# Gate and up of feed-forward block 0 by Strassen's seven block products, inner tiles taken 4, 6, 6, 6 at a time

## The chip, the cores and the metric

One core of one Trainium2 chip runs the whole program. The metric is the device time in microseconds, the median of several runs. TensorE (PE) multiplies and accumulates into PSUM, in eight banks of 128 x 512 fp32; VectorE (DVE), ScalarE (ACT) and GpSimd (POOL) work element by element; SyncE (SP) issues most DMAs. Each engine takes its instructions in the order in which they were queued and waits on semaphores of the others.

## The reference

Two transformer layers run over 256 context and 256 latent tokens (512 columns here), model width 1024, hidden width 2816 (22 tiles of 128). Layer 0 mixes by retention and a state-space scan, layer 1 by latent attention. Each layer ends in a gated feed-forward block; the change is in that of layer 0:

```
h = h + m[2] * mixer(modulate(rms_norm(h), m[0], m[1]))
h = h + m[5] * swiglu(modulate(rms_norm(h), m[3], m[4]), w_gate, w_up, w_down)
def swiglu(h, w_gate, w_up, w_down):
    return (jax.nn.silu(h @ w_gate) * (h @ w_up)) @ w_down
```

The m are conditioning vectors, separate for context and latent tokens, made from a condition by another matrix. All of it is fp32.

## The kernel before, in words

Activations lie with model channels on partitions and the 512 tokens along the row: `x[k]`, k = 0 to 7. To keep fp32 accuracy, each operand is cut into a high part (`wh`, `xh`, cast by ScalarE) and a low rest (`wl`, `xl`, subtracted by VectorE, for a few units by GpSimd), and each product is three matmuls: wh·xh, wh·xl, wl·xh (`mm3`, L231 to L234).

The `Feed` object brings all weights in a fixed order: SP loads a `raw` tile of up to 1 MB (a pool of four buffers), and each unit of 512 columns is then split into `wh` (L153) and `wl` (L154). `get(la)` hands out the next unit and has the splits queued `la` units ahead. Every other tile of 512 columns comes from one pool, `heap`, of 76 buffers.

Feed-forward block 0 (`ffn`) takes the 22 inner tiles in two halves of 11. For one inner tile, two products of eight contraction steps give gate and up (2 x 8 x 3 = 48 matmuls of 512 columns; the first two tiles together, while `x` is still being made); ScalarE takes silu of the gate (`sg`, L1290), VectorE multiplies by up (L1291), and the product is cut into `hdh` and `hdl` (L227, L228). After 11 tiles, the down projection runs over the eight output tiles: 33 matmuls each, and two residual additions to `h` on VectorE (L1195, one input in PSUM). The last output tile of the block is done in two halves of the tokens by `bridge`, which also makes the next layer's norm (`ms`, L337) and its first input.

A second stream on VectorE, `vec_all`, makes the conditioning vectors of layer 1: 96 steps that multiply a row of weights by the condition and add it up (`vo`, L503). Its generator is advanced NVS = 5 steps after each inner tile; its weights come as 1 MB loads into `raw`.

The order of the instructions on each engine is set by a list scheduler from the order of the program and its own costs; only `bridge` and the start of the norm are held in program order on TensorE.

## Time and profile before

| | |
|---|---|
| median of 3 runs | 1129.97 us (1129.36 to 1131.19) |
| profiled execution | 1133.19 us |
| its span, first to last instruction | 1131.4 us |
| mean granted TensorE clock | 0.976 |
| busy: TensorE, VectorE, ScalarE, GpSimd | 1081.2 (96%), 727.7 (64%), 493.2 (44%), 203.4 (18%) us |
| block 0's gate, up and down, about | 390 to 732 us of the span |

In a row of the windows view stand the stretch, its length, the busy time of PE, weight loads, DVE, ACT and POOL with their instruction counts, the granted clock, the DMA share and GB/s. A timeline row has start, duration, engine, line, operation, output<-inputs, form and count, and in brackets how long its engine sat idle before it and what released it. Matmul durations overlap, so the price of one is the step from start to start.

### The profile page before, as it was taken

How to read it: one execution, taken by the hardware profiler on the slowest of the kernel's cores; microseconds unless marked ns; L12 is line 12 of the kernel's file. 1: busy time of each engine (PE TensorE's matmuls, PEld its weight loads, DVE VectorE, ACT ScalarE, POOL GpSimd, SP SyncE). 2: the span in 40 equal slices, each digit the busy share in tenths (PEclk: the TensorE clock that was granted, in tenths of full speed). 3: DMA queues.
4: the chain of work that ended last, by engine and by line, in shares of the span. 5: the costliest groups of instructions: out<-in, count | busy, mean ns of one | idle time of the engine just before them, and what ended most of it. 6: DMA issues, size and time to landing. Idle time of an engine off the chain costs nothing.

```text
span 1131.4 us, 17225 instructions
## 1 busy us (share of the span) xinstructions
PE 1081.2 (96%) x6537; PEld 894.4 (79%) x6537; DVE 727.7 (64%) x1547; ACT 493.2 (44%) x991; POOL 203.4 (18%) x201
## 2 busy tenths in 40 slices
PE   8899999797998899999999999989999999999997
PEld 7687666565787688888888888858988779999996
DVE  4479499756646776663275753475888767574565
ACT  4372465745333533232132322344766645453442
POOL 2123154642022300000000000342232241000001
PEclk8999999898999899999999999999999989999998
DMA  9642797012362334354135546322343563473441
GB/s 348 227 150 88 241 324 243 38 38 75 112 223 76 112 123 175 125 190 150 38 114 222 203 174 227 123 75 80 90 126 105 194 224 122 145 288 135 163 154 38
DMA packets 42962, 172.43 MB, mean 152 GB/s; under 512 B 5472, under 2 KB 7152, under 8 KB 30720
## 3 DMA queue, kind: packets, MB, share of 16 engines
q1 hardware_dynamic: 42448, 170.69, 42.8%
q8 instruction: 51, 0.84, 0.3%
q10 hardware_dynamic: 432, 0.66, 0.2%
q14 instruction: 31, 0.25, 0.1%
HBM read 167.08 MB, written 1.10 MB: 149 GB/s over the span
## 4 chain that ended last, share of the span: by engine, by line
PE 59%; DVE 6%; ACT 2%; issue 1%; DMA 1%; DVEq 0%; SPq 0%; ACTq 0%
PE g L232 18%; PE g L234 17%; PE g L233 17%; PE ya L1521 1%; DVE wl L154 1%; PE ad L427 1%; DVE xl L543 1%; ACT wh L153 1%; DVE na L542 1%; PE tp L1512 1%; ACT xh L541 1%; PE st L334 1%; DVE mx L1500 1%; PE rb L321 0%; ACT P L1503 0%
## 5 line engine op out<-in xcount | busy, mean ns | idle before, releaser
L233 PE MATMUL g<-xl,wh 128*128 128x512 f32 (+1 forms) x968 | 337.1, 349 | 10.4 <-DVE xl L543 6.8
L232 PE MATMUL g<-xh,wh 128*128 128x512 f32 (+1 forms) x968 | 336.9, 351 | 2.4 <-ACT xh L541 2.4
L234 PE MATMUL g<-xh,wl 128*128 128x512 f32 (+1 forms) x968 | 334.7, 346 | 0.0
L154 DVE TENSOR_TENSOR wl<-raw,wh 128x512 fp32r<-128x512 f32 (+2 forms) x371 | 247.9, 711 | 59.5 <-ACT wh L153 57.2
L153 ACT CAST wh<-raw 128x512 fp32r<-128x512 f32 (+3 forms) x412 | 223.7, 597 | 54.1 <-PE g L233 30.5
L233 PEld LDWEIGHTS g<-xl,wh 128*128 128x128 f32 x968 | 183.7, 190 | 37.1 <-DVE xl L543 9.5
L232 PEld LDWEIGHTS g<-xh,wh 128*128 128x128 f32 x968 | 182.7, 190 | 37.3 <-issue 10.1
L234 PEld LDWEIGHTS g<-xh,wl 128*128 128x128 f32 x968 | 183.7, 190 | 24.3 <-issue 0.8
L365 POOL TENSOR_TENSOR sq<-sq 128x256 f32<-128x256 f32 (+1 forms) x30 | 31.0, 1032 | 616.7 <-ACT sq L361 614.8
L232 PE MATMUL g<-hdh,wh 128*128 128x256 f32 (+1 forms) x363 | 120.7, 333 | 0.0
L234 PE MATMUL g<-hdh,wl 128*128 128x256 f32 (+1 forms) x363 | 120.5, 332 | 0.0
L233 PE MATMUL g<-hdl,wh 128*128 128x256 f32 (+1 forms) x363 | 120.5, 332 | 0.0
L227 ACT CAST hdh<-sg 128x512 fp32r<-128x512 f32 (+1 forms) x44 | 22.6, 513 | 174.6 <-DVE sg L1291 174.6
L1291 DVE TENSOR_TENSOR sg<-sg,g 128x512 f32<-128x512 f32 (+1 forms) x44 | 24.4, 554 | 112.1 <-PE g L234 111.5
L233 PEld LDWEIGHTS g<-hdl,wh 128*128 128x128 f32 x363 | 68.3, 188 | 7.3
L234 PEld LDWEIGHTS g<-hdh,wl 128*128 128x128 f32 x363 | 68.3, 188 | 7.3
L232 PEld LDWEIGHTS g<-hdh,wh 128*128 128x128 f32 x363 | 68.3, 188 | 7.3
L1195 DVE SCALAR_TENSOR_TENSOR h<-g,mod,h 128x256 f32<-128x256 f32 x72 | 32.3, 479 | 60.0 <-PE g L234 59.8
L154 POOL TENSOR_TENSOR wl<-raw,wh 128x512 fp32r<-128x512 f32 (+1 forms) x41 | 56.6, 1385 | 51.5 <-ACT wh L153 43.1
L1290 ACT ACTIVATE sg<-g 128x512 f32<-128x512 f32 (+1 forms) x44 | 21.5, 488 | 72.3 <-PE g L234 72.2
L361 ACT ACTIVATE sq<-h 128x256 f32<-128x256 f32 (+1 forms) x30 | 15.5, 518 | 82.0 <-DVE h L1195 69.0
L228 DVE TENSOR_TENSOR hdl<-sg,hdh 128x512 fp32r<-128x512 f32 (+1 forms) x44 | 24.6, 559 | 25.4 <-ACT hdh L227 24.9
(307 smaller groups left out, 1706.6 us busy)
## 6 DMA issues: line engine op xcount, KB each, us to landing
raw<-in_wgu_dram SPq DMA_DIRECT2D x44, 1024.0 KB, 4.8
raw<-in_wdn_dram SPq DMA_DIRECT2D x32, 704.0 KB, 4.4
vr<-in_wav_dram SPq DMA_DIRECT2D x16, 1024.0 KB, 4.9
ar<-in_wad_dram SPq DMA_DIRECT2D x12, 1024.0 KB, 6.1
ar<-in_wad_dram SPq DMA_DIRECT2D x48, 256.0 KB, 6.4
raw<-in_win_dram SPq DMA_DIRECT2D x9, 1024.0 KB, 5.1
pc<-in_wad_dram SPq DMA_DIRECT2D x32, 256.0 KB, 6.6
raw<-in_wo_dram SPq DMA_DIRECT2D x8, 1024.0 KB, 4.8
```

The costliest lines, as they stand in the source:

```text
L153: self.nc.scalar.copy(hi[:, 0:n], src)
L154: (eng or (self.nc.gpsimd if self.ns in self.pool else self.nc.vector)).tensor_tensor(lo[:, 0:n], src, hi[:, 0:n].bitcast(F32), op=ALU.sub ...
L227: ACT.copy(hi[:, c0:c1], x[:, c0:c1])
L228: DVE.tensor_tensor(lo[:, c0:c1], x[:, c0:c1], hi[:, c0:c1].bitcast(F32), op=ALU.subtract)
L232: PE.matmul(ps, wh, xh, start=first, stop=False)
L233: PE.matmul(ps, wh, xl, start=False, stop=False)
L234: PE.matmul(ps, wl, xh, start=False, stop=last)
L361: ACT.activation(q[:, c0:c1], x[:, c0:c1], AF.Square)
L365: POOL.tensor_tensor(self.acc[0][:, c0:c1], self.acc[0][:, c0:c1], q[:, c0:c1], op=ALU.add)
L1195: DVE.scalar_tensor_tensor(out=h[k][:, a:b], in0=ps[:, a:b], scalar=mod[l][:, gate * 8 + k, r:r + 1], in1=h[k][:, a:b], op0=ALU.mult, op1= ...
L1290: ACT.activation(sg[:, c0:c1], pg[:, c0:c1], AF.Silu)
L1291: DVE.tensor_tensor(sg[:, c0:c1], sg[:, c0:c1], pu[:, c0:c1], op=ALU.mult)
```

## The change

The inputs of block 0's gate and up are taken as 2 x 2 blocks: weights [gate; up] by halves of the contraction (four blocks of 512 in each `raw` tile: gate k 0 to 3 at column 0, up k 0 to 3 at 512, gate k 4 to 7 at 1024, up k 4 to 7 at 1536), activations by halves of the contraction and by alternate 128-token pieces of each stream. Inner tiles 0 and 1 are computed as before. From tile 2 on, `seven` makes seven products of 4 contraction steps and 256 columns (7 x 4 x 3 = 84 matmuls) in three PSUM banks R, X and Y: t2 into X, b11 into R, t1 onto X, t3 into Y, b21 onto R, b22 onto X, t4 onto Y. Between them ScalarE copies X (`p6`) and R (`p1`), GpSimd adds these two (`u2`), VectorE makes `u4`, both halves of `nu` (up, from Y) and `c12` (the second half of the gate, from X), and ScalarE takes silu of R and of `c12`.

Four of the seven weight blocks are sums: GpSimd makes s1 to s4 from the `raw` tile, s2 from s1 and s4 from s2. The activations' sums are made once by `combine`, on VectorE and GpSimd, and one `raw` buffer holds their high parts to the end of the block. The down projection now follows groups of 4, 6, 6 and 6 inner tiles, so that it adds to `h` four times. The conditioning stream takes three steps after each down tile in place of five after each inner tile, and loads 64 pieces of 256 KB into `heap` tiles, two ahead.

```diff
+NVS = 3
+LV = 2
+PH0 = (4, 6, 6, 6)
+LW = 4
+WSUM = ("s2", 0, "s1", "s3", 512, "s4", 1536)
...
+    def sums(self, li, key):
+        if (li, key) not in self.sum:
+            add = lambda o, a, b: self.nc.gpsimd.tensor_tensor(o[:, 0:512], a, b, op=ALU.add)
+            r = self.raw[li]
+            t = self.sum[li, key] = self.tile(key, F32)
+            if key == "s1":
+                add(t, r[:, 1024:1536], r[:, 1536:2048])
+            elif key == "s2":
+                add(t, self.sums(li, "s1"), r[:, 0:512])
+            elif key == "s3":
+                add(t, r[:, 0:512], r[:, 1024:1536])
+            else:
+                add(t, self.sums(li, "s2"), r[:, 512:1024])
+        return self.sum[li, key][:, 0:512]
...
+    def combine(x, whole):
+        keep = rawp.tile([128, 2112], F32R, tag="raw", name="tk")
...
+        for j in range(4):
+            (b11, b12), (b21, b22) = halves(whole[j]), halves(whole[j + 4])
+            ta, tb = T("ta"), T("tb")
+            DVE.tensor_tensor(pair(ta[:, 0:256]), b11, b12, op=ALU.subtract)
+            DVE.scalar_tensor_tensor(out=pair(ta[:, 256:512]), in0=b22, scalar=-1.0, in1=pair(ta[:, 0:256]), op0=ALU.mult, op1=ALU.subtract)
+            POOL.tensor_tensor(pair(tb[:, 0:256]), b22, b12, op=ALU.subtract)
+            DVE.scalar_tensor_tensor(out=pair(tb[:, 256:512]), in0=pair(ta[:, 256:512]), scalar=-1.0, in1=b21, op0=ALU.mult, op1=ALU.subtract)
+            for n, t in (("t1", ta), ("t3", tb)):
+                hi, lo = keep[:, 512 * j:512 * j + 512] if n == "t1" else T("th", F32R), T("tl", F32R)
+                ACT.copy(hi, t)
+                DVE.tensor_tensor(lo, t, hi.bitcast(F32), op=ALU.subtract)
...
+    def seven(f):
+        R, X, Y = B("wr")[:, 0:256], B("wx")[:, 0:256], B("wy")[:, 0:256]
+        def prod(ps, n, first, last=False):
+            wh, wl = feed.get(LW)
+            for k in range(4):
+                xh, xl = f[n][k]
+                w = slice(k * 128, k * 128 + 128)
+                mm3(pair(ps), wh[:, w], wl[:, w], xh, xl, first and k == 0, last and k == 3, True)
+        p, u, sg, nu = T("p"), T("u"), T("sg"), T("nu")
+        p6, p1, u2, u4 = p[:, 0:256], p[:, 256:512], u[:, 0:256], u[:, 256:512]
+        prod(X, "t2", True)
+        ACT.copy(p6, X)
+        prod(R, "b11", True)
+        ACT.copy(p1, R)
+        POOL.tensor_tensor(u2, p1, p6, op=ALU.add)
+        prod(X, "t1", False)
+        DVE.tensor_tensor(u4, X, p1, op=ALU.add)
+        prod(Y, "t3", True)
+        DVE.tensor_tensor(halves(nu)[1], pair(Y), pair(u4), op=ALU.add)
+        prod(R, "b21", False, True)
+        ACT.activation(halves(sg)[0], pair(R), AF.Silu)
+        prod(X, "b22", False, True)
+        c12 = T("c12")[:, 0:256]
+        DVE.tensor_tensor(c12, X, p1, op=ALU.add)
+        ACT.activation(halves(sg)[1], pair(c12), AF.Silu)
+        prod(Y, "t4", False, True)
+        DVE.tensor_tensor(halves(nu)[0], pair(Y), pair(u2), op=ALU.add)
+        return sg, nu
...
+        for i, n in enumerate(PH0):
+            hid = []
+            for _ in range(n):
...
+                    sg, nu = seven(f)
+                    DVE.tensor_tensor(sg, sg, nu, op=ALU.mult)
+                hid.append(split(sg, "hd"))
...
+            for k in range(8):
+                if m == 22 and k == 7:
+                    return last(hid, n, 0, 5, so)
+                residual(k, gemm(hid, n), 0, 5, BOTH)
...
+                vec_step(NVS)
```

How the order on the engines moves is seen at three places. In the rows the numbers behind `s_` tell the sums apart; lines are those of each kernel's own file.

Place 1, VectorE in the middle of a group, around one inner tile. Before:

```order
L503 ISA va 128x1
L154 TENSOR_TENSOR wl<-raw,wh 128x512 x4
L1291 TENSOR_TENSOR sg<-sg,g 128x512
L228 TENSOR_TENSOR hdl<-sg,hdh 128x512
L503 ISA vo,mod_76<-vr,cb,va 128x512
```

Now (s_4614 is s2 and s_4615 s1 of the next tile, s_4671 its s3; L1402 is `u4`, L1404 and L1412 the halves of `nu`, L1409 `c12`):

```order
L185 TENSOR_TENSOR wl<-raw,wh 128x512
L1402 TENSOR_TENSOR u<-wx,p 128x256
L185 TENSOR_TENSOR wl<-s_4614,wh 128x512
L1404 TENSOR_TENSOR nu<-wy,u 128x2x128
L185 TENSOR_TENSOR wl<-raw,wh 128x512
L185 TENSOR_TENSOR wl<-s_4615,wh 128x512
L1409 TENSOR_TENSOR c_4668<-wx,p 128x256
L1412 TENSOR_TENSOR nu<-wy,u 128x2x128
L185 TENSOR_TENSOR wl<-s_4671,wh 128x512
L1437 TENSOR_TENSOR sg<-sg,nu 128x512
L267 TENSOR_TENSOR hdl<-sg,hdh 128x512
```

The splits now stand between operations that free PSUM banks, and those of s2, s1 and s3 come behind GpSimd.

Place 2, the same tile on ScalarE and on GpSimd. ScalarE before, then ScalarE now (s_4614 as above; `hdh` is that of this tile, the two copies those of the next):

```order
L1290 ACTIVATE sg<-g 128x512
L227 CAST hdh<-sg 128x512
L153 CAST wh<-raw 128x512 x4
L1290 ACTIVATE sg<-g 128x512
L227 CAST hdh<-sg 128x512
```

```order
L184 CAST wh<-s_4614 128x512
L184 CAST wh<-raw 128x512
L1406 ACTIVATE sg<-wr 128x2x128
L184 CAST wh<-s_4615 128x512
L1410 ACTIVATE sg<-c_4668 128x2x128
L184 CAST wh<-s_4671 128x512
L266 CAST hdh<-sg 128x512
L184 CAST wh<-raw 128x512
L1397 COPY p<-wx 128x256
L1399 COPY p<-wr 128x256
```

GpSimd, which had next to nothing in this stage before, now (L1400 is `u2` of a tile, the four sums behind it are those of the next):

```order
L1400 TENSOR_TENSOR u<-p 128x256
L157 TENSOR_TENSOR s_4615<-raw 128x512
L157 TENSOR_TENSOR s_4614<-s_4615,raw 128x512
L157 TENSOR_TENSOR s_4671<-raw 128x512
L157 TENSOR_TENSOR s_4719<-s_4614,raw 128x512
```

The copies of a tile's first two products stand behind the `hdh` of the tile before, and the next tile's sums behind the addition of these copies.

Place 3, VectorE where a down group ends and the next gate begins. Before:

```order
L1195 SCALAR_TENSOR_TENSOR h<-g,mod_75,h 128x256 x2
L154 TENSOR_TENSOR wl<-raw,wh 128x512
L1195 SCALAR_TENSOR_TENSOR h<-g,mod_75,h 128x256 x2
L1291 TENSOR_TENSOR sg<-sg,g 128x512
L228 TENSOR_TENSOR hdl<-sg,hdh 128x512
```

Now, after the group of four tiles; all 16 residual additions of the group stand ahead of this piece, and the first conditioning step of the group behind the eleventh of them:

```order
L544 ISA vo,mod_76<-vr,cb,va 128x512
L544 ISA mod_76 128x1
L185 TENSOR_TENSOR wl<-s_4385,wh 128x512
L544 ISA vo,va<-vr,cb,badj 128x512
L544 ISA va 128x1
L544 ISA vo,va<-vr,cb,badj 128x512
L544 ISA va 128x1
L544 ISA vo,mod_76<-vr,cb,va 128x512
L544 ISA mod_76 128x1
L185 TENSOR_TENSOR wl<-raw,wh 128x512
L185 TENSOR_TENSOR wl<-s_4470,wh 128x512
L1402 TENSOR_TENSOR u<-wx,p 128x256
```

The conditioning steps stand between the splits of the first tile of the next group, three to each, and ahead of its first `u4`.

More of the change, by code (lines that the diff above doesn't have):

```diff
@@ L137, in add, with add_sums @@
             c += n
+    def add_sums(self, ap):
+        li = len(self.loads)
+        self.loads.append((ap, 2048))
+        for c in WSUM:
+            self.last[li] = len(self.units)
+            self.units.append((li, c, 512))
+    def sums(self, li, key):
[12 more added lines that the diff above has]
+        return self.sum[li, key][:, 0:512]
     def load_to(self, li):
@@ L157, in split_to @@
                 del self.raw[li]
+                for key in [k for k in self.sum if k[0] == li]:
+                    del self.sum[key]
                 self.load_to(li + LD)
@@ L204, in hybrid_kernel @@
         feed.add(wo0[l], K8 * 2)
-    def add_ffn(i):
-        for half in range(2):
-            for m in range(11):
-                feed.add(wgu[i, half * 11 + m], K8 * 2, FPF if half == 0 and m < 3 else ())
-            for m in range(8):
-                feed.add(wdn[i, half * 8 + m], [512, 512, 384])
-    add_ffn(0)
+    m = 0
+    for i, n in enumerate(PH0):
+        for _ in range(n):
+            if m < 2:
+                feed.add(wgu[0, m], K8 * 2, FPF)
+            else:
+                feed.add_sums(wgu[0, m])
+            m += 1
+        for k in range(8):
+            feed.add(wdn0[i * 8 + k][:, 0:128 * n], [512, 128 * n - 512] if n > 4 else [128 * n])
     for l in range(4):
@@ L220, in hybrid_kernel @@
         feed.add(wo1[l], K8 * 2)
-    add_ffn(1)
+    for half in range(2):
+        for m in range(11):
+            feed.add(wgu[1, half * 11 + m], K8 * 2, FPF if half == 0 and m < 3 else ())
+        for m in range(8):
+            feed.add(wdn[half * 8 + m], [512, 512, 384])
     def split(x, nm, cols=(0, 512)):
```

114 lines of the change are left out of this document (79 added, 35 removed).

## The prediction

> **What bounds the kernel now.** I read the engine totals of the page first (TensorE 96% busy, in the table above), then the windows for the gate, up and down stage of block 0 (390 to 732 us), then the timeline inside it. Behind the window's length come the busy times of TensorE, its weight loads, VectorE, ScalarE and GpSimd, then the granted clock and the DMA share.
>
> ```profile
> 390.00:732.00 342.00, 341.63 (x1487) 277.19 (x1487) 194.10 (x399) 98.77 (x183) 8.70 (x7) 1.00 0.43 154
> ```
>
> TensorE is busy 341.6 of 342 us at full clock; VectorE 194, GpSimd 9. So TensorE bounds the stage, and a matmul saved here shortens the kernel only as far as VectorE, ScalarE and GpSimd keep up with what they get in exchange. By the table above the span is 1131.4, this execution's time 1133.19 and the median 1129.97; I work out a difference in span and add it to the median.
>
> The price of a matmul is the step between two starts. The first pair of rows is this stage, the second the same stage of block 1:
>
> ```profile
> 394.62 0.40 PE L232 MATMUL g<-xh,wh 128*128 128x512 f32 x1
> ...
> 401.80 0.39 PE L233 MATMUL g<-xl,wh 128*128 128x512 f32 x1
> ...
> 959.84 0.28 PE L233 MATMUL g<-xl,wh 128*128 128x256 f32 x1
> ...
> 962.09 0.28 PE L234 MATMUL g<-xh,wl 128*128 128x256 f32 x1
> ```
>
> 31 steps make 7.18 us: 0.2316 us for 512 columns. 19 steps make 2.25: 0.1184 for 256.
>
> **Removed.** In 20 of 22 inner tiles, 48 matmuls of 512 columns (11.12 us) become 84 of 256 (7 products x 4 x 3; 9.95 us). That is 1.17 us a tile, **-23.4 us** in all. The 528 down matmuls stay. Three of the seven products read their moving operand as two runs of 128 columns, which no row shows; I take 0.1184 because the column count is the same, and keep the price of 512 as a rival.
>
> **Added on the other engines.** The durations, from the timeline and from groups by form (count, busy, mean ns):
>
> ```profile
> 399.55 0.68 DVE L1291 TENSOR_TENSOR sg<-sg,g 128x512 f32<-128x512 f32 x1
> ...
> 400.26 0.62 ACT L227 CAST hdh<-sg 128x512 fp32r<-128x512 f32 x1 [5.75 <-DVE sg L1291]
> ...
> 400.79 2.18 ACT L153 CAST wh<-raw 128x512 fp32r<-128x512 f32 x4
> ...
> 401.52 2.49 DVE L154 TENSOR_TENSOR wl<-raw,wh 128x512 fp32r<-128x512 f32 x4
> ...
> 405.91 0.75 DVE L503 CUSTOM_DVE_ANT_0 vo<-vr,cb,badj 128x512 f32<-128x512 f32 x1
> ...
> L365 POOL TENSOR_TENSOR sq<-sq 128x256 f32<-128x256 f32 x16 | 12.1, 758 | 204.4 <-ACT sq L361 202.7 <-DVE wl L154 1.5
> ...
> L1291 DVE TENSOR_TENSOR sg<-sg,g 128x256 f32<-128x256 f32 x22 | 9.3, 421 | 39.0 <-PE g L234 38.4 <-ACT sg L1290 0.4
> ```
>
> A VectorE subtraction costs 0.62 in a row of four, a ScalarE cast 0.55, one conditioning step (vo) 0.75, a 256-column VectorE operation 0.42, a GpSimd one 0.76. For a ScalarE copy of 256 columns I take VectorE's 0.42 too, since the casts and subtractions of 512 above are alike (0.55 and 0.62). A Strassen tile then has on VectorE nine operations of 512 and four of 256: 9 x 0.62 + 4 x 0.42 = 7.3 us; on ScalarE about 6; on GpSimd four sums of 1.29 (row below) and one of 0.76: 5.9. Each fits into 9.95. They are not independent, though:
>
> ```profile
> 327.80 2.04 DVE L1195 SCALAR_TENSOR_TENSOR h<-g,mod,h 128x256 f32<-128x256 f32 x5
> ...
> 340.60 4.71 DVE L154 TENSOR_TENSOR wl<-raw,wh 128x512 fp32r<-128x512 f32 x4
> ...
> 329.01 4.04 POOL L365 TENSOR_TENSOR sq<-sq 128x512 f32<-128x512 f32 x3 [51.70 <-ACT sq L361]
> 335.98 1.29 POOL L365 TENSOR_TENSOR sq<-sq 128x512 f32<-128x512 f32 x1 [2.92 <-ACT sq L361]
> ...
> 341.50 1.54 POOL L365 TENSOR_TENSOR sq<-sq 128x512 f32<-128x512 f32 x1 [2.96 <-ACT sq L361]
> 343.00 1.78 POOL L154 TENSOR_TENSOR wl<-raw,wh 128x512 fp32r<-128x512 f32 x1
> ```
>
> Four subtractions took 4.71 instead of 2.49 while two GpSimd operations ran: **1.1 us lost per GpSimd operation**, and those two took 0.25 and 0.49 longer than 1.29. The five residual additions, with one input in PSUM, took 0.41 each beside GpSimd: nothing lost. [...]
>
> **The loop through four queues** (places 1 and 2 of the order rows). In the middle of a group each tile m hands to the next: product t4 (12 x 0.1184, and 0.16 until the last one's 0.28 is over: 1.58), nu 0.42, the split of s3 0.62, sg 0.68; ScalarE hdh 0.62, a weight cast 0.55, the copies of X and R 0.42 + 0.42, queued behind hdh; GpSimd u 0.76, s1 1.29, s2 1.29; ScalarE's cast of s2 0.62, VectorE's split of s2 0.62, and behind that the other nu 0.42, which the next t4 waits for since it frees bank Y. Sum 10.3, with 13 hand-overs of 0.03 (400.23 to 400.26) 10.7 us. With locks: s1 and s2 0.74 longer, s4 against the two splits beside t4 1.1, s3 against the split of s2 about 0.3: 12.8. Five of the sixteen tiles that have a successor in their group run sg ahead of the split, 0.62 less. Against 9.95 the excess is 0.75 to 2.85 (0.13 to 2.2 for the five), 9 to 42 us. I take 1.5, since both engines are busy over half the time: 15 tiles (the sixteenth lies in the next term), **+22 us** (8 to 40).
>
> **The pile-up after the first down group** (place 3). The residual pair's price and two places where VectorE's lead shows:
>
> ```profile
> 691.52 0.87 DVE L1195 SCALAR_TENSOR_TENSOR h<-g,mod,h 128x256 f32<-128x256 f32 x2 [3.82 <-PE g L234]
> ...
> 382.72 0.69 DVE L543 TENSOR_TENSOR xl<-na,xh 128x512 fp32r<-128x512 f32 x1
> 383.33 1.28 DVE L154 TENSOR_TENSOR wl<-raw,wh 128x512 fp32r<-128x512 f32 x2
> 390.33 0.69 DVE L1291 TENSOR_TENSOR sg<-sg,g 128x512 f32<-128x512 f32 x1 [5.71 <-PE g L234]
> ...
> 733.66 0.48 DVE L1195 SCALAR_TENSOR_TENSOR h<-g,mod,h 128x256 f32<-128x256 f32 x1 [0.32 <-PE g L234]
> 736.48 0.16 DVE L337 TENSOR_SCALAR ms<-st 128x2 f32<-128x2 f32 x1 [2.34 <-PE st L334]
> ```
>
> The first conditioning step stands behind a residual addition of the sixth output tile. From there to the addition that frees bank X in tile 4, VectorE has 5 residual operations (0.44), 23 steps (0.75) and 9 splits (0.62): 25.0 us. TensorE needs that bank after two down tiles (24 x 0.2316 = 5.6) and five products (5 x 1.42): 12.7. TensorE waits 12.3; four sums of the next tile may lock 4.4 more. I take **+13** (11 to 17).
>
> **The combinations before the first product.** Today VectorE is through at 384.6 and then waits 5.7 us for TensorE. The change puts two more splits (1.24) and 20 operations there, 4 x (3 x 0.42 + 2 x 0.62) = 10; the product t2 needs all but the last. Done at 395.2. TensorE ends its first group at about 389.6 (390.33 less a silu of some 0.6 and the hand-overs) and could run three quarters of t2, 1.06: 4.5 late, up to 9 with the locks of four sums and four GpSimd subtractions, 4 if operations follow each other as the splits do. **+6** (4 to 9).
>
> **The bridge to block 1.** Today ms follows the residual by 2.8 us. Now seven steps and four splits (7.7) stand between, an eighth ahead of the second half, and VectorE arrives late: 4.0 an output tile (two splits 1.0, residuals 0.87, three steps 2.2), plus half a lock, against 18 x 0.2316 = 4.17. **+6** (2 to 10).
>
> **The rest.** The two later down groups need 4.0 of 4.17 and the next tile's sums: +1 each (0 to 3). The group of four has 9 x 0.2316 = 2.1 of cover for its last hidden tile, which takes 2.0 to 2.7 after the last product: 0.5 (0 to 1). Loads cost nothing: the weight bytes are the same, the stage's DMA share is 0.43, and the conditioning rows, now in 64 pieces of 256 KB, are issued two pieces ahead, which is 1.4 us and more of VectorE work. If that cover is too thin, each piece can hold VectorE for up to its time to landing (this row's last number), and with it the splits behind it:
>
> ```profile
> h<-in_xin_dram SPq DMA_DIRECT2D x16, 256.0 KB, 5.5
> ```
>
>
> **Sum:** -23.4 + 22 + 13 + 6 + 6 + 2.5 = +26: 1130 + 26 = **1156 us**. All low ends give +2, all high ends +60.
>
> **The rivals.** *The exchange works*: VectorE, ScalarE and GpSimd interleave inside 9.95, and of the pile-up and the ends some 8 us stay: -23.4 + 8, 1115 us. For it: each engine alone has 2.6 us or more of room per tile. Against it: the loop is longer than 9.95 even without a lock. Chance 0.20. *Locks at every sum*: the loop runs at 12.8 and the ends at their worst: 1190. For it 4.71 against 2.49; against it the four PSUM operations of a tile, which do not lock. Chance 0.17. *Gain and waits cancel*: low ends, +2, 1132. Chance 0.09. *Strided columns cost more*: 720 matmuls at the price of 512, 720 x 0.113 = +81. The loop then hides behind TensorE and the other waits, 27, stay: -23.4 + 81 + 27, 1215. Nothing speaks for it but that no row shows it. Chance 0.02. My forecast has the remaining 0.52.
>
> **How the numbers follow.** A measurement of this kernel tells about 0.2% (2.3 us) from no change. Faster takes the first rival, 0.20; same takes 0.05 of the third; slower the rest, 0.75. The range reaches from just above the first rival's time, 1118, to 1183; the forecast's own is 1138 to 1178.
>
> **What would show it.** In the changed kernel's windows: TensorE busy 80 to 90% in gate and up, a tile period of 11 to 12 us, VectorE above 80%. In the timeline: splits beside GpSimd sums near 1.7 us, and a VectorE run of some 25 us of steps after the first down group with TensorE waiting on DVE wl or DVE u. In the waits: PE wy behind DVE nu. Wrong would be a tile period of 10 with TensorE solid; then GpSimd's sums run ahead and the loop is not closed.

## The result, and the profile after

The changed kernel takes 1212.8 us (median of 4 runs, 1210.2 to 1216.9) against 1129.7 (1128.7 to 1131.2) for the kernel before on the same chip: 1.074 times as long, 95% interval 1.070 to 1.077. The forecast of slower was right; its 1156 us and its range up to 1183 were not. The profiled execution has a span of 1209.7 us, 78.3 more than before, and the rest of this text follows these 78.3.

The windows view of the changed kernel, cut at its own stages (columns as in the prediction: stretch, length, busy time of PE, weight loads, DVE, ACT and POOL, granted clock, DMA share, GB/s):

```profile
387.50:401.70 14.20, 0.95 (x6) 0.93 (x5) 10.78 (x21) 7.96 (x14) 0.00 (x0) 0.64 0.00 1
401.70:425.50 23.80, 21.98 (x169) 21.61 (x169) 12.93 (x23) 9.13 (x20) 7.48 (x6) 0.93 0.15 45
...
448.80:478.00 29.20, 14.37 (x86) 13.52 (x85) 26.45 (x53) 5.80 (x12) 9.48 (x6) 0.77 0.42 146
478.00:537.70 59.70, 52.15 (x423) 50.28 (x421) 45.59 (x66) 27.48 (x60) 29.02 (x21) 1.00 0.19 62
...
571.00:588.80 17.80, 12.52 (x86) 12.31 (x85) 15.01 (x27) 4.12 (x9) 7.42 (x5) 0.83 0.20 72
588.80:648.80 60.00, 52.34 (x422) 50.59 (x422) 45.65 (x66) 27.58 (x60) 28.59 (x21) 0.99 0.18 62
...
682.10:699.80 17.70, 12.02 (x85) 11.56 (x84) 15.71 (x27) 4.36 (x10) 7.41 (x5) 0.81 0.28 92
699.80:759.50 59.70, 52.07 (x423) 50.31 (x422) 45.65 (x66) 27.58 (x60) 29.00 (x21) 1.00 0.20 69
759.50:819.80 60.30, 47.04 (x249) 37.52 (x247) 41.89 (x99) 15.26 (x31) 13.03 (x9) 0.83 0.79 282
```

The rows are, in order: the gap between the end of the first group (tiles 0 and 1) and the first of the seven products; tiles 2 and 3; the first tile after the first down group; five more tiles; the first tile and the five more of the next two groups; the last down group with the bridge, up to the first product of layer 1. The two down groups in between (33.3 us each, not shown) are solid. TensorE, busy 341.6 of 342 us before, now stands still in every one of these rows, and where it stood for 5 us the clock column falls too (0.64, 0.77, 0.83, 0.81 and 0.83, against 0.99 to 1.00 in the three rows of five tiles).

The kernel before, the 11 tiles of its second half and then its last down group with the bridge:

```profile
553.70:676.00 122.30, 122.30 (x530) 99.18 (x529) 71.78 (x156) 33.44 (x61) 0.00 (x0) 1.00 0.45 165
676.00:744.50 68.50, 67.82 (x383) 55.47 (x381) 29.89 (x60) 18.52 (x36) 12.45 (x9) 1.00 0.49 164
```

Stage by stage, after less before (us of span):

| stage | before | after | difference |
|---|---|---|---|
| up to the end of the first group | 391.6 | 387.5 | -4.1 |
| gap before tile 2 | 0.7 | 14.1 | +13.4 |
| 20 tiles: matmuls alone (9.95 against 11.12 each) | 222.5 | 199.1 | -23.4 |
| 17 of the tiles, over 9.95 | | | +34.0 |
| the first tile after each of three down groups, over 9.95 | | 29.2, 17.8, 17.7 | +34.9 |
| down groups and bridge | 61.2 + 68.5 | 23.3 + 33.3 + 33.4 + 60.3 | +20.6 |
| layer 1 | 386.9 | 389.9 | +3.0 |

The first and the last row nearly cancel; they are not followed further.

Two prices of the prediction can be read off at once. Here are the starts of the product with the strided operand (`wr`) and of the one behind it:

```profile
572.39 0.28 PE L272 MATMUL wr<-xh,wh 128*128 128x256 f32 x1
...
573.81 0.28 PE L272 MATMUL wy<-th,wh 128*128 128x256 f32 x1
```

Twelve matmuls in 1.42 us: 0.118 each, as assumed, so the gain of 23.4 us is there and the rival "strided columns" is out. And the groups by form, 385 to 815 us, answer to the 0.62 and 1.29 of before (mean ns behind the comma):

```profile
L185 DVE TENSOR_TENSOR wl<-raw,wh 128x512 fp32r<-128x512 f32 x95 | 93.8, 989 | 9.8 <-ACT wh L184 9.8
...
L185 DVE TENSOR_TENSOR wl<-s,wh 128x512 fp32r<-128x512 f32 x77 | 65.3, 848 | 33.1 <-ACT wh L184 33.1
L157 POOL TENSOR_TENSOR s<-s,raw 128x512 f32<-128x512 f32 x38 | 61.4, 1615 | 12.5 <-PE wx L273 4.1 <-DVE va L544 2.7 <-PE g L273 2.2
...
L157 POOL TENSOR_TENSOR s<-raw 128x512 f32<-128x512 f32 x38 | 58.4, 1538 | 88.4 <-PE g L273 49.8 <-DMA raw<-in_wgu_dram 15.8 <-DVE va L544 10.4
```

A split takes 0.85 to 0.99 us on average and a sum 1.54 to 1.62: beside each other both engines are slower, as in the kernel before (4.71 us against 2.49 for four splits), but in every tile of the stage.

(A slip in the part on the change, on which no number rests: of the four blocks of a `raw` tile the second is gate k 4 to 7 and the third up k 0 to 3.)

### The profile page after: what moved, and what is told of

Read it like the earlier page. It is cut to its first block, busy times and chain, and to the rows that moved or that the text cites. A ratio compares the mean times of both kernels' runs of the same rounds, so it can differ in the third digit from the quotient of the medians.

```text
span 1209.7 us, 19402 instructions
## 1 busy us (share of the span) xinstructions
PE 1081.7 (89%) x7242; PEld 928.6 (77%) x7242; DVE 873.8 (72%) x1750; ACT 546.6 (45%) x1127; POOL 344.8 (28%) x303
## 3 DMA queue, kind: packets, MB, share of 16 engines
q1 hardware_dynamic: 51664, 170.69, 40.5%
## 4 chain that ended last, share of the span: by engine, by line
PE 31%; DVE 11%; issue 6%; POOL 2%; ACT 2%; DMA 1%; SPq 0%; DVEq 0%; POOLq 0%; ACTq 0%
PE g L274 8%; PE g L272 8%; PE g L273 7%; DVE wl L185 3%; DVE vo L544 2%; POOL s L157 2%; PE ya L1659 1%; ACT wh L184 1%; PE tp L1650 1%; DVE na L583 1%; DMA vr<-in_wav_dram 1%; DVE h L1236 1%; PE as L272 1%; PE as L274 0%; PE as L273 0%
## 5 line engine op out<-in xcount | busy, mean ns | idle before, releaser
L185 DVE TENSOR_TENSOR wl<-raw,wh 128x512 fp32r<-128x512 f32 (+3 forms) x361 | 270.9, 782 | 37.8 <-ACT wh L184 35.6
L273 PE MATMUL g<-xl,wh 128*128 128x256 f32 (+1 forms) x648 | 211.5, 327 | 8.2 <-DVE xl L584 4.6
L272 PE MATMUL g<-xh,wh 128*128 128x256 f32 (+1 forms) x648 | 212.4, 332 | 4.5 <-ACT xh L582 4.5
L274 PE MATMUL g<-xh,wl 128*128 128x256 f32 (+1 forms) x648 | 209.6, 324 | 0.0
L272 PEld LDWEIGHTS g<-xh,wh 128*128 128x128 f32 x648 | 123.9, 193 | 26.5 <-issue 10.7
L273 PEld LDWEIGHTS g<-xl,wh 128*128 128x128 f32 x648 | 124.8, 193 | 20.3 <-DVE xl L584 6.8
L274 PEld LDWEIGHTS g<-xh,wl 128*128 128x128 f32 x648 | 124.6, 192 | 10.1 <-issue 0.8
L185 DVE TENSOR_TENSOR wl<-s,wh 128x512 fp32r<-128x512 f32 x80 | 67.8, 848 | 33.1 <-ACT wh L184 33.1
L157 POOL TENSOR_TENSOR s<-raw 128x512 f32<-128x512 f32 x40 | 61.1, 1528 | 88.4 <-PE g L273 49.8
L157 POOL TENSOR_TENSOR s<-s,raw 128x512 f32<-128x512 f32 x40 | 64.3, 1608 | 12.5 <-PE wx L273 4.1
```

Of the source, the lines that this page charges most:

```text
L157: add = lambda o, a, b: self.nc.gpsimd.tensor_tensor(o[:, 0:512], a, b, op=ALU.add)
L185: (eng or (self.nc.gpsimd if self.ns in self.pool else self.nc.vector)).tensor_tensor(lo[:, 0:n], src, hi[:, 0:n].bitcast(F32), op=ALU.sub ...
L272: PE.matmul(ps, wh, xh, start=first, stop=False, skip_group_check=skip)
L273: PE.matmul(ps, wh, xl, start=False, stop=False, skip_group_check=skip)
L274: PE.matmul(ps, wl, xh, start=False, stop=last, skip_group_check=skip)
```

## Reading the four losses in the trace

**The tiles.** One tile of the middle of a group, timeline rows of four engines (GpSimd, ScalarE, VectorE, TensorE):

```profile
605.33 0.78 POOL L1400 TENSOR_TENSOR u<-p 128x256 f32<-128x256 f32 x1 [5.62 <-ACT p L1399]
606.08 1.73 POOL L157 TENSOR_TENSOR s<-raw 128x512 f32<-128x512 f32 x1
607.89 1.62 POOL L157 TENSOR_TENSOR s<-s,raw 128x512 f32<-128x512 f32 x1
...
603.57 0.62 ACT L266 CAST hdh<-sg 128x512 fp32r<-128x512 f32 x1 [1.42 <-DVE sg L1437]
...
604.88 0.37 ACT L1399 COPY p<-wr 128x256 f32<-128x256 f32 x1
...
609.54 0.62 ACT L184 CAST wh<-s 128x512 fp32r<-128x512 f32 x1 [3.25 <-POOL s L157]
...
610.20 1.13 DVE L185 TENSOR_TENSOR wl<-s,wh 128x512 fp32r<-128x512 f32 x1 [1.50 <-ACT wh L184]
611.25 0.41 DVE L1404 TENSOR_TENSOR nu<-wy,u 128x256 f32<-128x256 f32 x1
...
611.81 0.36 PE L272 MATMUL wy<-th,wh 128*128 128x256 f32 x1 [1.31 <-DVE nu L1404]
```

This is the loop as predicted, link by link: `hdh` of the last tile, copy `p1` queued behind it, `u2`, `s1`, `s2`, the cast, the split, `nu`, product t4. GpSimd stands idle 5.62 us until `p1` comes, although the sums behind `u2` need nothing of this tile. The period is 11.4 to 12.8 us: 12.7 to 12.8 where `wl` of `s3` comes ahead of `sg` in the tile before, 11.4 to 11.8 in the others.

**The first tile after a down group.** VectorE and TensorE after the second one:

```profile
575.76 1.70 DVE L185 TENSOR_TENSOR wl<-s,wh 128x512 fp32r<-128x512 f32 x1
577.39 1.77 DVE L544 CUSTOM_DVE_ANT_0 vo<-vr,cb,badj 128x512 f32<-128x512 f32 x1
...
579.09 1.75 DVE L544 CUSTOM_DVE_ANT_0 vo<-vr,cb,badj 128x512 f32<-128x512 f32 x1
...
580.76 1.74 DVE L544 CUSTOM_DVE_ANT_0 vo<-vr,cb,va 128x512 f32<-128x512 f32 x1
...
583.04 0.41 DVE L1402 TENSOR_TENSOR u<-wx,p 128x256 f32<-128x256 f32 x1
...
577.94 0.28 PE L274 MATMUL wr<-xh,wl 128*128 128x256 f32 x1
583.50 0.58 PE L272 MATMUL wx<-xh,wh 128*128 128x256 f32 x1 [5.28 <-DVE u L1402]
...
589.43 0.35 PE L272 MATMUL wx<-tk,wh 128*128 128x256 f32 x1
```

Three conditioning steps left over from the down group and a split among them are each stretched from 0.74 or 0.68 to 1.70 to 1.77 by the next tile's four sums: 4.1 us. TensorE waits 5.28 for `u4` behind them. Then it runs slowly: the 27 steps from 583.50 to 589.43 make 0.22 us each in place of 0.118, 2.7 us more. 5.3 and 2.7 are, but for 0.1, the 7.9 that this tile takes over 9.95.

**The gap.** ScalarE behind the combinations, and the wait of TensorE:

```profile
396.06 0.62 ACT L1371 CAST th<-tb 128x512 fp32r<-128x512 f32 x1
396.70 1.28 ACT L1429 ACT_TABLE_LOAD   x1
397.99 0.60 ACT L1429 ACTIVATE sg<-g 128x512 f32<-128x512 f32 x1
399.35 0.62 ACT L266 CAST hdh<-sg 128x512 fp32r<-128x512 f32 x1 [0.76 <-DVE sg L1430]
399.87 0.59 ACT L1429 ACTIVATE sg<-g 128x512 f32<-128x512 f32 x1
400.36 0.36 ACT L474 COPY adev<-ad 128x256 f32<-128x256 f32 x1
```

```profile
PE ad L485 <- ACT adev L474: 13.2, 1, 13.2
```

```profile
391.99 0.61 PE L445 MATMUL ad<-prm,adev 128*128 128x8 f32 x4 [0.37 <-ACT adev L434]
```

(The second fence is the waits view: in total, times, longest. The third is the kernel before.) The combinations end near 397.4; the silus of tiles 0 and 1 stand behind them on ScalarE, and the copy `adev` behind these; 1.28 us of it is a table load that ScalarE makes ahead of the first silu. A matmul of the other conditioning stream, `ad`, stands ahead of t2 in TensorE's queue and waits for that copy. Before, the same `ad` waited 0.37 us (third fence).

**The bridge.** The waits that count between 759 and 820 us:

```profile
PE g L274 <- DVE wl L185: 7.3, 3, 4.0
DVE vo L544 <- DMA vr<-in_wav_dram: 7.3, 2, 4.5
...
PE st L374 <- DVE ms L377: 5.9, 2, 5.6
```

VectorE waits for pieces of the conditioning weights (`vr`), and TensorE for splits and for the norm (`ms`) queued behind these steps.

## The experiments

Each was profiled; those with an interval were also timed in several rounds. "Bridge" is the stretch from the start of the last down group to the first product of layer 1 (before: 68.5 us, 7.4 more than its 61.1 of matmuls; after: 60.3 us, 27 more than its 33.3), "first tiles" are those after the three down groups (after: 29.2, 17.8, 17.7), "middle tiles" four in each of the three later groups (after: 11.4 to 12.8, mean 12.2). A single time can be off by 0.6% (the kernel before took 1125.6, 1131.2 and 1132.3 beside them), so the stages decide.

### The weight sums left out (e1)

```diff
-            src = self.sums(li, c0) if isinstance(c0, str) else self.raw[li][:, c0:c0 + n]
+            c0 = {"s1": 1024, "s2": 1536, "s3": 1024, "s4": 1536}.get(c0, c0)
+            src = self.raw[li][:, c0:c0 + n]
```

> Leaves out the four weight sums on GpSimd: the raw block that was its first or second operand stands in place of each sum, so gate and up of 20 inner tiles are not the reference's; products, splits, copies and conditioning steps stay. Theory (the loop runs through GpSimd's sums, and the sums slow VectorE): tiles in the middle of a group fall from 11.5 to 12.8 us to 10.0 to 10.5, the first tiles after the down groups from 29, 18 and 18 us to about 24, 14 and 14; time 1165 to 1175. Rival (the loop is closed by VectorE's and ScalarE's queues without the sums, the copies behind hdh): the middle tiles stay above 11.3 us, time above 1190.

Measured: 1154.6 us (before beside it 1125.6). Middle tiles 9.9 to 10.4, mean 10.06; first tiles 23.8, 10.3, 10.3; the bridge as it was (60.0), the gap nearly (12.0). The theory holds, and the gain is larger than it said: 58 us go with the sums (54 by the ratios to the kernel before). Four middle tiles in the windows view:

```profile
559.30:599.80 40.50, 40.25 (x338) 39.88 (x337) 30.58 (x52) 22.39 (x48) 3.85 (x4) 1.00 0.22 74
```

TensorE is solid, and VectorE is busy 7.65 us a tile.

### The conditioning steps left out (e2), and then only their length (e10)

```diff
-        for n in range(LV):
-            load(n)
+        for l, c, nr in VEC_CHUNKS:
+            DVE.memset(mod[l][:, 8 * c:8 * c + 8, 0:nr], 0.0)
+        units = []
```

> Leaves out the 96 conditioning steps on VectorE and their 64 loads (shift and scale of layer 1 are zero instead). Theory (the first tiles of the groups and the bridge wait for a VectorE that drains these steps): the first tiles after the down groups fall from 29, 18 and 18 us to about 13 each, the bridge gives back some 12 to 16 of the 20 us that it lost, the middle tiles stay at 11.5 to 12.8; time 1160 to 1172. Rival (those tiles are long because GpSimd's sums for them come late): they stay above 16 us, time above 1190.

Measured: 1164.9 us (1125.6). First tiles 11.1, 11.0, 11.1; bridge 41.8, that is 18.5 us given back; middle tiles 11.6 to 12.8. The theory holds, and both places gave back more than it said. To tell the steps' time on VectorE from their loads, the next kernel keeps both, but lets a step work on 2 columns:

```diff
-                DVE.tensor_tensor_reduce(out=T("vo"), in0=w, in1=cb[r][q], ...
+                DVE.tensor_tensor_reduce(out=S("vo", 2), in0=w[:, 0:2], in1=cb[r][q][:, 0:2], ...
```

> Keeps the 64 loads of the conditioning weights and the 96 steps, but a step multiplies 2 columns in place of 512, so that it costs VectorE some 0.1 us (the conditioning of layer 1 is not the reference's). Theory (VectorE's time in these steps makes the first tiles and the bridge long): first tiles 11 to 12 us, and from the start of the last down group to the first product of layer 1 some 42 us as without steps and loads, in place of 60; time 1162 to 1170. Rival (the loads, at a DMA share of 1.0 in the bridge, are late themselves or hold up the other weights): that stretch stays above 52 us, time above 1175.

Measured: 1184.3 us (1131.2). Here theory and rival are right in one place each. The first tiles fall (17.9, 11.0, 11.1): these are the steps' time. (The first is still 8 us over 9.95, since VectorE is not idle there from 442 to 465 us: a short step takes 0.14 us, up to 1.3 beside a sum, and there are some two dozen of them.) The bridge does not fall: 59.2. Its waits with the short steps, 737 to 797 us:

```profile
DVE vo L544 <- DMA vr<-in_wav_dram: 17.7, 10, 4.2
...
PE st L374 <- DVE ms L377: 12.6, 2, 12.3
```

VectorE stands ten times for a piece that has not landed, and `ms` stands behind it. So the loads alone are enough to make the bridge that long; the steps at full length without their loads were not run. The stretch moves 60.3 us x 282 GB/s = 17 MB after (row above), before 68.5 x 164 = 11 MB; between 780 and 790 us the DMA engines of the changed kernel are full:

```profile
780.00:790.00 10.00, 5.40 (x23) 3.73 (x21) 8.13 (x17) 4.28 (x9) 4.52 (x4) 1.00 1.03 406
```

The cover of two pieces is the same in the two down groups before. There a piece lands in 3.5 and 4.1 us (median), at a DMA share of 0.68 and 0.71, and VectorE never waits for one; in the bridge, where layer 1's own weights are loaded too, it takes 7.2 us. No run loads further ahead, so it stays open whether a deeper cover would have been enough.

### Grouping and moved steps without the seven products (e5)

```diff
-                    sg, nu = seven(f)
+                    pg, nu = gemm(x, 8), gemm(x, 8)
+                    sg = T("sg")
+                    ACT.activation(sg, pg, AF.Silu)
```

(and no sums, no combinations, no change of sign.)

> Groups of 4, 6, 6 and 6 and conditioning steps behind the down tiles, but all 22 inner tiles as plain gate and up products of eight steps: no sums, no combinations, no seven products. Theory (the loss comes from the sums, the combinations and VectorE's load in the Strassen tiles): tiles at 11.1 us, a few us lost behind the down groups (the 23 steps are drained while a plain tile asks little of VectorE), the bridge 10 to 16 us longer than before: time 1140 to 1155. Rival (four down groups and the moved steps are the cost themselves): 1170 or more.

Measured: 1155.1 us (1125.6), the theory's upper edge. The tiles are solid at 11.1, the first ones too; the bridge takes 60.6, some 20 us more than before where the theory allowed 16:

```profile
705.00:765.60 60.60, 46.64 (x248) 36.89 (x246) 38.13 (x96) 14.50 (x29) 13.72 (x9) 0.83 0.77 267
```

So the loss in the bridge has nothing to do with the seven products; with plain tiles, VectorE takes the left-over steps without a wait of TensorE.

### The steps back behind the inner tiles (e3)

```diff
-NVS = 3
+NVS = 5
...
                 hid.append(split(sg, "hd"))
+                if m != 1:
+                    vec_step(NVS)
...
-                vec_step(NVS)
```

> Undoes one part of the change alone: five conditioning steps after each inner tile as before, none in the down groups; the seven products, their sums and the groups of 4, 6, 6, 6 stay, and nothing is left out. Theory (VectorE has 9.4 us of work with its losses in a Strassen tile, and 3.75 more do not fit): the bridge gives back some 18 us and the first tiles some 20, but the middle tiles grow from 12.2 to 13 or 14: 1190 to 1205. Rival (the steps fit into VectorE's idle time in the tiles): tiles stay near 12.2, time 1165 to 1178.

Measured: 1223.2 us (1130.1). The bridge is at 41.7 and the first tiles at 11.1, as the theory said, but the middle tiles take 16.6 to 18.4, far more than it said:

```profile
PE wr L274 <- DVE wl L185: 62.5, 15, 5.5
```

Fifteen waits of some 4 us each: five steps stand in one piece ahead of a split that a product needs, and the granted clock in these tiles is 0.80 (after: 0.99 to 1.00). Moving the steps out of the tiles was the lesser loss.

### The gap: the place of `ad` (e4), and work to cover it (f1, f4)

First `ad` and `adev` two tiles later:

```diff
-                        mid()
-                        DVE.tensor_scalar(out=g, in0=g, scalar1=-1.0, ...)
...
+                if m == 3:
+                    mid()
+                    DVE.tensor_scalar(out=g, in0=g, scalar1=-1.0, ...)
```

> Moves the last piece of the other conditioning stream (ad, L485, and its ScalarE copy adev) from behind inner tile 1 to behind inner tile 3; nothing is left out. Theory (TensorE stands at ad, whose copy is queued behind the silus of tiles 0 and 1, 3 us longer than the combinations need): the gap before the first product falls from 13.5 to about 10 us; time 1208 to 1210. Rival (the combinations' low parts are what the product waits for): the gap stays at 13 or more.

Measured: 1212.2 us, no change. TensorE began t2 at once and then waited piece by piece: from the end of the first group to the first down group 37.7 us in place of 38.0. Neither line describes it: without `ad` in the way, TensorE met the casts of the combinations, then the copy `p6` behind the silus on ScalarE (4.2 us), then `ad` in its new place (3.1).

Then tile 2 plain, to give TensorE work meanwhile:

```diff
+PLAIN = (2,)
...
-            if m < 2:
+            if m < 2 or m in PLAIN:
...
+                elif m in PLAIN:
+                    pg, pu = gemm(x, 8), gemm(x, 8)
```

> Inner tile 2 as a plain product of 48 matmuls between the first group and the first Strassen tile, and the ad piece behind it; nothing is left out. Theory (TensorE has nothing to do while VectorE and ScalarE make the combinations): TensorE runs on for 11 us where it stood 13.5, and 1 to 3 us of the gap stay for ScalarE's silus; 1.2 us of the seven products' gain is given up: time 1198 to 1203. Rival (the same waits come behind tile 2, as VectorE and ScalarE get the work of one more tile): 1207 or more.

Measured: 1206.4 us (1131.2), nearly the rival's; the stretch, which now holds tile 2's 11.1, is 33.5, since `ad`, now behind tile 2, waits 9.6 us for its copy, which ScalarE has behind three silus, seven casts and the table load. With tile 2 plain and `ad` and `adev` put ahead of the combinations:

```diff
+                        mid()
+                        DVE.tensor_scalar(out=g, in0=g, scalar1=-1.0, ...)
                         f = combine(x, whole)
```

> Tile 2 plain as in the run before, but the ad piece and its copy adev ahead of the combinations instead of behind two silus; nothing is left out. Theory (the 9.6 us that TensorE stood at ad behind plain tile 2 came from the place of the copy in ScalarE's queue): the gap falls below 2 us, time 1196 to 1199. Rival (the first Strassen tile waits for its operands or copies anyway): 4 us and more of gap stay, 1201 or more.

Measured: 1195.8 us (1132.3). The gap is gone, the stretch 25.4 (21.1 would be solid); tile 3 is longer (14.4). The theory holds: cover and place of `ad` together give back 12.6 us of this stretch, where the one alone gave 0.3 and the other 4.5.

### The loop: splits earlier (e6), `u2` off GpSimd (e7), sums off GpSimd (e8)

```diff
-LW = 4
+LW = 8
```

> Weight pieces are split 8 ahead of their product in place of 4 (LW); nothing is left out, and GpSimd makes the first two sums of a tile ahead of the addition u2 of the tile before, in place of behind it. Four sums a tile still stand beside VectorE. Theory (the loop: p6, p1, u2, s1, s2, cast, split, nu, t4 hands each tile to the next): the middle tiles fall to 10.2 to 10.8 us, time 1175 to 1190. Rival (VectorE's time lost beside GpSimd is the bound, whatever the order): they stay at 11.5 or more, time 1200 or more.

Measured: 1206.6 us (1131.2), middle tiles 12.0 on average. The rival's number, but not its reason: the trace shows `u2` still ahead of `s3` and `s4` in GpSimd's queue, idle 5 to 6 us before it. The experiment did not open the loop. The next one does:

```diff
-        POOL.tensor_tensor(u2, p1, p6, op=ALU.add)
+        DVE.tensor_tensor(u2, p1, p6, op=ALU.add)
```

> One line: the addition u2 (of the two copies p1 and p6) goes from GpSimd to VectorE, so that no operation in GpSimd's queue waits for the tile in progress any more; the four sums stay on GpSimd and beside VectorE. With splits 8 ahead the tiles came down only to 11.9, but there u2 still stood in GpSimd's queue ahead of the sums s3 and s4 that the next split waits for. Theory (the loop goes through u2 and GpSimd's order): middle tiles 10.0 to 10.8 us, time 1175 to 1190. Rival (VectorE's loss beside GpSimd's sums is the bound): 11.5 or more, time above 1200.

Measured: 1189.1 us (1132.3), middle tiles 9.9 to 12.1, mean 10.6, though VectorE got more to do. One operation of 0.8 us in the wrong queue was worth some 24 us. What is left is another bound:

```profile
585.10:627.40 42.30, 40.51 (x338) 40.04 (x337) 40.50 (x56) 21.89 (x48) 21.41 (x14) 1.00 0.20 70
```

VectorE is busy 40.5 of 42.3 us, 10.1 a tile, where the kernel without sums had 7.65. Of the 2.5 between, 0.4 is `u2` and about 2 is time that VectorE loses beside the four sums. With the sums on VectorE itself:

```diff
-            add = lambda o, a, b: self.nc.gpsimd.tensor_tensor(...)
+            add = lambda o, a, b: self.nc.vector.tensor_tensor(...)
```

> One word: the four weight sums go from GpSimd to VectorE, u2 stays on GpSimd. VectorE gets 4 x 0.62 = 2.5 us more work per tile, 9.8 in all, and next to nothing stands beside it on GpSimd. Theory of the loop through GpSimd: without hand-overs and losses the tiles come to 10 to 10.8 us, the first tiles of the groups fall by some 3 us each, time 1175 to 1190. Rival (VectorE has too little time for 9.8 us of work in its order): tiles of 11.5 to 12.5, time 1200 or more.

Measured: 1194.3 us (1132.3), middle tiles 10.4 to 11.8, mean 11.6 (from `b11` to `b11`, since the tiles overlap here): the rival on the tiles, the theory nearly on the time. The first tiles fell (22.7, 12.5, 15.2, counted alike). VectorE is busy 10.1 us a tile, as in e7, with a period one us longer, so its order counts beside its sum. The sums cost VectorE about as much where they are (2 us lost) as if it made them (2.5).

### Everything together (f3, f5, f6, f8 to f11)

First, in f3, the remedies of e6 and f1 with the steps spread: their preparation ahead of the combinations, one or two steps behind an inner tile, 1, 2, 2, 0 behind a down tile, so that the bridge has neither steps nor loads; the last 32, needed only by layer 1's feed-forward, behind the bridge.

```diff
+NVS = (1, 2, 2, 0)
+NVT = (0, 0, 2, 1, 1, 1, 1, 1, 1, 1, 1, 1, 1, 1, 1, 1, 2, 2, 2, 2, 2, 2)
...
+                vec_step(NVT[m])
...
-                vec_step(NVS)
+                vec_step(NVS[i])
```

> All of it: tile 2 plain and ad behind it, splits 8 ahead, and the conditioning steps spread anew: their preparation before the combinations, then 1 to 2 steps after each inner tile and 1, 2, 2, 0 after each down tile of the four groups, the last 32 (for layer 1's feed-forward) behind the bridge; nothing is left out. Theory (loop, pile-ups, gap and bridge are separate and each is undone): gap about 2 us, middle tiles 10.3 to 11, first tiles 11 to 12, bridge as before: -23 plus 10 to 25 against the kernel before, 1115 to 1132. Rival (VectorE is short of time in all, and what is moved comes back in the tiles): tiles of 11.5 and more, 1145 or more.

Measured: 1180.3 us (1131.2): first tiles 10.9, 11.9, 11.8, but middle tiles of 11 to 15, TensorE's wait for `ad` still 13.4 (tile 2 plain, `ad` behind it), and `u2` still on GpSimd. The next kernel, f5, takes three remedies over from above: `u2` on VectorE, `ad` ahead of the combinations, the spread steps; tile 2 stays plain.

> The four remedies together, nothing left out: u2 on VectorE, tile 2 plain with the ad piece ahead of the combinations, the conditioning steps at 1 to 2 an inner tile and 1, 2, 2, 0 a down tile with their preparation ahead of the combinations, the last 32 of them behind the bridge. The earlier run with the steps spread like this, but u2 on GpSimd and ad behind tile 2, took 1180. Theory (the losses add up): 25 us less for the loop and 12 for the gap, 1140 to 1150. Rival (VectorE, over 90% busy in the tiles, is now the bound, and the steps in the tiles cost what the loop gave): 1155 or more.

Measured: 1163.9 us, 1.031 (1.027 to 1.034) of the kernel before. The rival's number, with a cause that neither names: the 32 deferred steps stand on VectorE in one piece behind the bridge, and TensorE waits for layer 1's first input.

```profile
PE g L274 <- ACT xh L584: 22.8, 3, 20.9
```

(f3 lost about as much there.) The next kernel, f6, has this wait as well:

```diff
-on_k = project(xm, 0, 2, BOTH, tick=lambda k: hold(k, 3, sum(G0)), ...
+on_k = project(xm, 0, 2, BOTH, tick=lambda k: (vec_step(1 if k == 0 else 5 if k < 6 else 0), hold(k, 3, sum(G0))), ...
```

> As the run before, but with one step only in the inner tiles: some 25 conditioning steps go into the output projection of layer 0's mixer, ahead of block 0 (5 after each of its output tiles 1 to 5), where TensorE is busy throughout and VectorE 10 to 15 of 20 us. Nothing is left out. Theory (VectorE's time in the tiles is the bound by now, so a step taken out of a tile gives its 0.75 us and up to 1.1 more beside GpSimd): 15 to 25 us less than the run before, 1122 to 1135, about the time of the kernel before. Rival (the steps cost the same ahead of block 0, by its bridge): no less than the run before.

Measured: 1167.7 us, 1.034 (1.031 to 1.037). The 18 tiles of the three later groups took 195.8 us in place of 205.6, but the first group ended 17 us later than in f5: the steps and their loads cost in the bridge ahead of block 0 what they cost in the one behind it. The rival. So the deferred steps went one at a time into layer 1's attention, and tile 3 became plain too (f8):

```diff
-    for _ in vec_it:
-        pass
...
         ada_step(upto=5)
+        vec_step(1)
```

> As f5, with two corrections that its trace shows and nothing left out: the last 32 conditioning steps, which stood in one piece on VectorE behind the bridge (TensorE waited 21 us there), go one at a time into the attention of layer 1; tile 3 is plain too, since the first Strassen tile came while ScalarE still had the silus and splits of tiles 0 to 2 behind the combinations (31 us from the end of the first group to the first down group in place of 22). Six steps behind tile 3, one behind each later tile. Theory (the losses are separate places, and VectorE keeps up at 1 step a tile): 1164 less 21, less 9, less 5 for one step a tile in the last group: 1124 to 1135. Rival (VectorE is the common bound, and the steps put into the attention hold it up): 1140 or more.

Beside it, with fewer steps in the last group and more behind tiles 2 and 3 (f9):

```diff
-NVT = (0, 0, 0, 6, 1, 1, 1, 1, 1, 1, 1, 1, 1, 1, 1, 1, 1, 1, 1, 1, 1, 1)
+NVT = (0, 0, 4, 8, 1, 1, 1, 1, 1, 1, 1, 1, 1, 1, 1, 1, 0, 0, 0, 0, 0, 0)
```

> As f8, but no conditioning steps in the last six Strassen tiles; four more behind tile 2 and two more behind tile 3, which are plain. Theory (each step in a Strassen tile costs VectorE 0.75 us and more, and VectorE is over 90% busy there): 3 to 6 us less than f8. Rival (tile period is set by the loop of hand-overs, not by VectorE's sum): within 2 us of f8.

Measured: f8 1153.7 us, 1.022 (1.019 to 1.024), the best complete version; f9 1168.3 us, 1.034 (1.030 to 1.038). In f8 layer 1 begins at 746.2 us, 1.7 later than in the kernel before: block 0 is nearly level. Then layer 1 takes 20 us more, with 20.7 us more work on VectorE. Windows of layer 1 in f8, then in the kernel before:

```profile
746.00:1153.00 407.00, 377.79 (x2854) 341.63 (x2846) 283.29 (x609) 203.94 (x439) 75.59 (x61) 0.97 0.44 151
```

```profile
744.00:1131.00 387.00, 371.36 (x2858) 338.63 (x2850) 262.61 (x547) 203.65 (x440) 73.41 (x61) 0.98 0.40 138
```

f9 tells that taking one step a tile away gains nothing here: the six last tiles take 66.5 us without, 65.1 with them. And twelve steps behind tiles 2 and 3 pile up again (first down group 30 us, the tile behind it 18.3).

The last two, f10 and f11, on what is left, both edits of f8:

```diff
         xbc.append(conv(c, xr[c]))
+        vec_step(6)
...
-tick=lambda k: hold(k, 3, sum(G0))
+tick=lambda k: (vec_step(4 if k < 3 else 0), hold(k, 3, sum(G0)))
```

> As f8, but the 32 steps that stood in layer 1's attention go ahead of block 0: 23 into the stage of layer 0 at 40 to 60 us of the span, where VectorE is busy 9 of 20 us, and 12 into the output projection at 300 to 330 us, where it is busy about half; nothing is left out. Theory (block 0 with the seven products costs as much as before by now, and only the steps for which block 0 has no room on VectorE cost the 22 us behind it): 1130 to 1140. Rival (VectorE has no free time at those places either, since its queue is what TensorE follows there): 1148 or more.

and, with the edit of the second experiment (the steps left out):

> As f8, but the 96 conditioning steps and their loads are left out (layer 1's shift and scale are zero). Theory (VectorE's time is the bound that is left: the seven products gain what VectorE can be freed of): tiles of 10.0 to 10.5 us and no wait behind the down groups, 1108 to 1118, that is 12 to 22 us below the kernel before. Rival (the hand-overs of the tiles keep their period at 11 or more whatever VectorE has to do): 1122 or more.

Measured: f10 1160.5 us, 1.027 (1.024 to 1.031): the steps put ahead of block 0 made the first group end 25 us later than in f8 (TensorE waited up to 16.5 us for a split behind them). f11, without any step: 1121.8 us, 0.993 (0.991 to 0.995). The middle tiles keep 10.4 to 11.5, mean 10.9, with VectorE at 94%:

```profile
539.80:583.20 43.40, 41.15 (x339) 40.15 (x337) 40.74 (x56) 21.85 (x48) 19.71 (x14) 1.00 0.19 67
```

For f10 the rival is right. For f11 neither line quite is: the time is the rival's edge, but the period is below 11, and VectorE is busy 10.2 us of 10.85. That it sets the period is argued, not shown: in e8 and f9 its sum alone did not. Against the kernel before with its steps, the seven products gain 8 us of their 21 (18 tiles x 1.17) with every conditioning step gone. (The kernel before without its steps was not run; with TensorE busy 341.6 of 342 us it had little to gain.)

## Why the prediction was too low, step by step

The direction and most of the waits were foreseen; the sizes were not. In the prediction's terms: the loop +34 (22 forecast), the first pile-up +19 (13), the two later ones together +16 (2), the combinations +13 (6), the bridge +20 (6). The two worst, some 14 us each, are terms that the prediction put at little or nothing: the sums that meet the last steps of the later groups, and the loads in the bridge.

- **Removed, -23.4:** right. 0.118 a matmul, strided or not.
- **The loop, "I take 1.5":** the mechanism right, the size low. Its own upper bound was 12.8 us a period where `wl` of `s3` comes ahead of `sg`; the tiles show 12.8 there and 11.4 to 11.8 for the others, against 12.2 with a loss at every sum and 10.1 without. 17 tiles lose 34 us in place of 22 for 15, and the last tile of a group, which the prediction left at 9.95, takes 11.0 to 11.1. The reason given for 1.5, that both engines are busy over half the time, was an average, where the row of four splits beside two GpSimd operations had already shown the loss. One line (e7) undid it. No run shows a lock; what the prediction calls one is a loss read off durations, 1.1 us of VectorE for each GpSimd operation beside it and 0.25 to 0.49 of that operation itself, and the changed kernel shows durations too: a split at 0.85 to 0.99 us (0.62 in the prediction's rows), a sum at 1.54 to 1.62 (1.29).
- **The pile-up, "+13" and "+1 each":** 19 for the first and 7.8 for each later group. Without sums it is 13.9 (e1): the working of steps, residuals and splits (12.3) was nearly right, and the rest goes with the sums: the losses beside GpSimd, allowed for in the 17 and not taken, and longer pauses with their slow matmuls. For the later groups the step failed: the sum of VectorE's work in a down group (4.0 of 4.17 a tile) left no room for the sums that meet its last steps. Without the steps or without the sums these tiles are at 10.3 to 11.1 (e1, e2): it takes both.
- **The combinations, "+6":** 13.4. Two things were not in the working: the combinations wait for ScalarE's casts and take 11.2 us, and the `ad` matmul with its copy behind two silus. Putting `ad` elsewhere alone gave nothing (e4); work for TensorE and `ad` ahead gave it back (f4).
- **The bridge, "+6":** some 18 to 20 with or without the seven products (e5). The step that failed is the one on the loads, "Loads cost nothing": it took the stage's mean DMA share of 0.43, where the bridge has its own, and the 23 pieces of that stretch came to a DMA at 1.0 (row at 780 us; e10 shows that the loads alone make the bridge that long). The sentence on a cover that is too thin, with 5.5 us a piece, named the mechanism and did not price it; here a piece took 7.2.
- **No term for the clock.** A pause of TensorE was counted with its length alone. In 385 to 830 us, the matmuls that ran while the trace's clock record stands at 0.5 took 15 us over the normal steps (0.118 or 0.232); in the kernel before the clock is 1.00 all through block 0. These 15 us are a part of the terms above: the pile-ups, the gap and the bridge.
- **The rivals:** "locks at every sum" (1190) had the loop right; all high ends together, +60, were still 18 short of 78.
- **What would show it:** period 11 to 12 predicted, 11.4 to 12.8 seen; TensorE 87% busy in the tiles (52.2 of 59.7; 80 to 90 predicted); VectorE above 80% predicted, 76% seen, since it waits inside the loop.

What stays open: whether another order of VectorE's queue (an order written out by hand in place of the scheduler's) would bring f8 below the kernel before. It wasn't tried. Shown is that no place that was tried takes the 96 steps for nothing once VectorE has the seven products' work, and that without the steps the gain is 0.7%.

## What to carry to other kernels

An exchange of TensorE's work for work on three other engines is not priced by their busy shares: follow one tile through the queues, and look for the operation that waits for this tile and stands ahead of operations that don't (`u2`: 0.8 us of work, some 24 us of time). A background stream that was free in one place has to be priced again where it is moved, its loads by the DMA share of that very stretch and its steps by what stands behind them in the queue. And a pause of TensorE of 4 to 6 us cost here a third to a half as much again in the slow matmuls that followed it (1.6 to 2.8 us).
